# RMSNorm with repeat: the two halves of the first tile on two hardware queues, gamma behind the first half

## The chip, the cores and the metric

The kernel runs on one core of a Trainium2 chip. The metric is the device time of one execution in microseconds. Times inside an execution are counted from the start of its span, which is some 1.8 us shorter than the device time.

## The reference, cut to what matters

```
x: (8, 512, 2048) float32, gamma: (2048,) float32, R = 2
x_rep  = repeat(x, 2, axis=1)
rms    = sqrt(mean(x_rep**2, axis=-1) + 1e-6)
out    = x_rep / rms * gamma            # (8, 1024, 2048) float32
```

Each row of x is normalised, scaled by gamma, and written twice. 33.6 MB are read and 67.1 MB written.

## The kernel before

The 4096 rows are cut into eight tiles of 128 partitions by four rows. A tile's loads put the four rows (8 KB each) into the second half of a buffer of eight rows; ScalarE squares and sums each row and takes the root, VectorE scales the row by the reciprocal and gamma into its place, and then the rows are copied to their doubles. One store writes the eight rows of each partition (64 KB). There are three buffers, so three tiles are loaded at first, and later loads wait for stores.

```
    def load(i, eng, parts=1):
        y = rows.tile([P, K * R, D], f32, name="y")
        step = K // parts
        for k in range(0, K, step):
            at = K * (R - 1) + k
            eng.dma_start(out=y[:, at : at + step, :], in_=x_t[i, :, k : k + step, :])
        ys.append(y)
    ...
    load(0, nc.sync, parts=2)
    gamma_b = singles.tile([P, D], f32, name="gamma_b")
    cuts = [0, *range(D // 4, D + 1, D // 8)]
    for c0, c1 in zip(cuts, cuts[1:]):
        nc.scalar.dma_start(out=gamma_b[0:1, c0:c1], in_=gamma[c0:c1].partition_broadcast(1))
    nc.gpsimd.partition_broadcast(out_ap=gamma_b[:], in_ap=gamma_b[0:1, :])
    eps_t = singles.tile([P, 1], f32, name="eps_t")
    nc.vector.memset(eps_t, eps)
    load(1, nc.sync)
    load(2, nc.sync)
    ...
    loads_after = {2: (3, 4, 5), 4: (6, 7)}
    for i in range(ntiles):
        compute(i)
        store(i, 0, K)
        for j in loads_after.get(i, ()):
            load(j, nc.sync)
```

Gamma comes in seven pieces on ScalarE's queue, with nothing ahead of it there; all x traffic is on SP's queue; and the only transfers queued before the first store are the loads of tiles 0, 1 and 2.

## Time and profile before

| | before |
|---|---|
| device time, median | 239.7 us in three runs; 239.45 us over all six runs beside the changed kernel |
| span of the profiled run | 237.9 us |
| broadcast of gamma starts | 12.60 us |
| first store issued | 27.05 us |
| last load of tiles 0 to 2 complete | 33.0 us |
| last store packet ends | 236.8 us |

The busy shares, the chain and the queues are read in the prediction. Here is one more view of the kernel before, the table of waits on the compute engines: who waited for whom, us in total, how often, the longest.

```profile
POOL gamma_b L96 <- DMA y<-in_x_dram: 12.2, 1, 12.2
DVE y L74 <- POOL gamma_b L96: 3.0, 1, 3.0
```

The first of these lines is an example of a wait that is put down to the wrong one. It names x, as if the broadcast had waited for the first tile. The program makes the broadcast wait for gamma alone; gamma's last completion packet (the 4-byte packet that follows a transfer's data in the packet records) came at 12.02 and the broadcast started at 12.60, while SP's second half of x completed only at 12.63. The chain of waits, shown in the prediction, names gamma. When a view names an input that the instruction does not read, look up the packets.

### The profile page before, as it was taken

The page shows a single profiled execution, that of the slowest core. Times are in us where ns is not written, and L with a number is a line of the kernel's source. Part 1 is how long each engine was busy: PE and PEld are TensorE (multiplying, and loading weights), DVE is VectorE, ACT ScalarE, POOL GpSimd, SP SyncE. Part 2 cuts the span into 40 slices and gives each one's busy share as a digit, 9 for nine tenths or more (in the row PEclk, how much of TensorE's full clock was granted, in tenths as well). Part 3 has the DMA queues.
Part 4 walks back from the last instruction along what each step waited for, and adds up shares of the span by engine and source line. Part 5 has one row for each costly group of instructions (what it writes and reads, how often), then busy time and mean ns, then how long its engine had stood idle before and what let it go on. Part 6 is the DMA issues. An engine that isn't in the chain of part 4 may idle for free.

```text
span 237.9 us, 287 instructions
## 1 busy us (share of the span) xinstructions
DVE 96.5 (41%) x73; ACT 101.0 (42%) x106; POOL 2.5 (1%) x5
## 2 busy tenths in 40 slices
DVE  0049999960000000059999960000199990000000
ACT  2697999900000000099999920000599960000000
POOL 0030000000000000000000000000000000000000
DMA  7999998989899998999998999989998989999994
GB/s 265 436 446 441 441 441 353 530 353 496 386 452 430 397 485 353 441 441 441 441 518 364 464 419 430 452 369 430 435 518 364 518 364 485 397 452 430 408 474 176
DMA packets 2464, 100.69 MB, mean 423 GB/s; under 512 B 279, under 2 KB 285, under 8 KB 286
## 3 DMA queue, kind: packets, MB, share of 16 engines
q1 hardware_dynamic: 2448, 100.66, 98.5%
q14 instruction: 2, 0.02, 0.0%
q10 hardware_dynamic: 14, 0.01, 0.0%
HBM read 33.56 MB, written 67.11 MB: 423 GB/s over the span
## 4 chain that ended last, share of the span: by engine, by line
DMA 58%; ACT 12%; DVE 9%; issue 1%; POOLq 1%; ACTq 1%; SPq 0%
DMA y<-in_x_dram 33%; DMA out_dram<-y 21%; ACT sq L64 8%; DVE y L74 7%; DMA gamma_b<-in_gamma_dram 4%; ACT y L81 3%; DVE y L81 2%; ACT rms L68 1%; POOLq L136 1%; ACTq L95 1%; DVE rstd L73 0%; POOLq L96 0%; SPq L56 0%
## 5 line engine op out<-in xcount | busy, mean ns | idle before, releaser
L64 ACT ACTIVATE sq<-y 128x2048 f32<-128x2048 f32 x32 | 59.7, 1865 | 87.8 <-DMA y<-in_x_dram 87.8
L74 DVE SCALAR_TENSOR_TENSOR y<-y,rstd,gamma_b 128x2048 f32<-128x2048 f32 x32 | 75.3, 2352 | 4.1 <-POOL gamma_b L96 3.0
L73 DVE RECIPROCAL rstd<-rms 128x1 f32<-128x1 f32 x32 | 5.0, 158 | 94.6 <-ACT rms L68 94.3
L81 ACT COPY y<-y 128x4096 f32<-128x4096 f32 x8 | 28.7, 3590 | 1.4 <-DVE y L74 1.4
L81 DVE COPY y<-y 128x4096 f32<-128x4096 f32 x8 | 18.3, 2294 | 0.3
L68 ACT ACTIVATE rms<-ss,eps_t 128x1 f32<-128x1 f32 x32 | 9.4, 295 | 1.0
L64 ACT ACTIVATION_READ_ACCUMULATOR sq<-y 128x1 f32 x32 | 6.0, 187 | 0.0
L64 ACT ACT_TABLE_LOAD x1 | 1.3, 1283 | 3.0 <-issue 3.0
L96 POOL PARTITION_BROADCAST gamma_b<-gamma_b x1 | 2.3, 2294 | 12.2 <-DMA y<-in_x_dram 12.2
L68 ACT ACT_TABLE_LOAD x1 | 1.3, 1283 | 0.0
L98 DVE MEMSET eps_t<- 128x1 f32 x1 | 0.1, 59 | 0.8 <-PEq L125 0.8
L125 POOL MEMSET const-uint8-127<- 128x1 uint8 x1 | 0.1, 102 | 0.0
L125 POOL MEMSET const-bfloat16-1.0<- 128x1 bf16 x1 | 0.1, 101 | 0.0
L125 POOL MEMSET const-float32-0.0<- 128x1 f32 x1 | 0.1, 98 | 0.2 <-issue 0.2
L125 POOL MEMSET const-float32-1.0<- 128x1 f32 x1 | 0.1, 98 | 0.0
## 6 DMA issues: line engine op xcount, KB each, us to landing
y<-in_x_dram SPq DMA_DIRECT2D x7, 4096.0 KB, 14.6
y<-in_x_dram SPq DMA_DIRECT2D x2, 2048.0 KB, 7.4
out_dram<-y SPq DMA_DIRECT2D x8, 24.4
gamma_b<-in_gamma_dram ACTq DMA_DIRECT2D x6, 1.0 KB
gamma_b<-in_gamma_dram ACTq DMA_DIRECT2D x1, 2.0 KB
```

The source lines that it names most:

```text
L64: nc.scalar.activation(out=sq[:], in_=ys[i][:, K * (R - 1) + k, :], func=Act.Square, accum_out=ss[:])
L68: nc.scalar.activation(out=rms[:], in_=ss[:], func=Act.Sqrt, scale=inv_d, bias=eps_t[:])
L73: nc.vector.reciprocal(out=rstd[:], in_=rms[:])
L74: nc.vector.scalar_tensor_tensor(out=ys[i][:, R * k, :], in0=ys[i][:, K * (R - 1) + k, :], scalar=rstd[:], in1=gamma_b[:], op0=Alu.mult, o ...
L81: copy(out=y_r[:, k0:k1, 1, :], in_=y_r[:, k0:k1, 0, :])
L95: nc.scalar.dma_start(out=gamma_b[0:1, c0:c1], in_=gamma[c0:c1].partition_broadcast(1))
L96: nc.gpsimd.partition_broadcast(out_ap=gamma_b[:], in_ap=gamma_b[0:1, :])
L98: nc.vector.memset(eps_t, eps)
L125: nc = _bacc.Bacc("TRN2", target_bir_lowering=False, num_devices=1)
L136: with _tile.TileContext(nc) as tc:
```

## The change

The intent is to send the two halves of the first tile out at once, one from each hardware queue, so that neither waits for the other to be issued. Since ScalarE's queue now begins with a half, gamma stands behind that half on it.

```diff
-    def load(i, eng, parts=1):
+    def load(i, queues):
         y = rows.tile([P, K * R, D], f32, name="y")
-        step = K // parts
-        for k in range(0, K, step):
+        step = K // len(queues)
+        for k, eng in zip(range(0, K, step), queues):
             at = K * (R - 1) + k
             eng.dma_start(out=y[:, at : at + step, :], in_=x_t[i, :, k : k + step, :])
 ...
-    load(0, nc.sync, parts=2)
+    load(0, (nc.scalar, nc.sync))
 ...                                   (gamma's seven pieces follow on nc.scalar, as before)
-    load(1, nc.sync)
-    load(2, nc.sync)
+    load(1, (nc.sync,))
+    load(2, (nc.sync,))
 ...
-            load(j, nc.sync)
+            load(j, (nc.sync,))
```

## The prediction

> **What bounds the kernel now.** I read the page first: its busy shares, the strip of 40 slices, and the queues.
>
> ```profile
> DVE 96.5 (41%) x73; ACT 101.0 (42%) x106; POOL 2.5 (1%) x5
> ...
> DMA  7999998989899998999998999989998989999994
> ...
> HBM read 33.56 MB, written 67.11 MB: 423 GB/s over the span
> ```
>
> No compute engine reaches half the span, and the DMA strip is full from the second slice to the last but one. The bytes decide: a 64 KB store packet takes 2.418 us in the trace's packet records, so 16 engines move about 434 GB/s and 100.7 MB need 232 us of the 237.9. The other 6 us are the start (first data packet at 1.73 us), the ramp (first packets of 16 KB take 0.7 to 1.6 us, later ones 0.611) and the end. A change to the first tile can therefore matter in two ways only: a few tenths at the start, or a **hole in the DMA stream**.
>
> So I next asked where a hole could open. The chain of waits, cut to the first 28 us:
>
> ```profile
> 2.69 9.71 DMA gamma_b<-in_gamma_dram
> ...
> 12.55 2.35 POOLq L136
> 14.90 0.02 issue
> 14.92 2.35 DVE y L74
> ...
> 24.69 2.30 DVE y L81
> ...
> 27.05 25.77 DMA out_dram<-y
> ```
>
> Read it downwards: gamma's last piece lands, GpSimd broadcasts it, VectorE scales four rows and copies two, and at 27.05 the first store is issued. This chain, and not x, sets the first store. Meanwhile the DMA engines work off the loads of tiles 0, 1 and 2, which are all that is queued until that store; the packet records show their last completion packet at 33.0. The store was thus queued about 6 us before the loads ran out, and there was no hole.
>
> Two more views matter. The waits of the issuing sequencer SP show waits that no data explains:
>
> ```profile
> SPq L52 <- DMA y<-in_x_dram: 5.7, 1, 5.7
> ...
> SPq L52 <- DMA gamma_b<-in_gamma_dram: 0.9, 1, 0.9
> ```
>
> The second half of x was issued only at 2.03, after gamma's first piece had landed, and tile 1 at 8.11, after the first half had landed. In the trace the DMA issues count on eight semaphores used in turn, and a ninth issue waits for the first user of its semaphore. And the queues between 5.6 and 12.1 us:
>
> ```profile
> q1 hardware_dynamic: 186, 2.79, 100.0%
> q10 hardware_dynamic: 12, 0.01, 0.3%
> ```
>
> q1 is SP's queue, q10 that of ScalarE, with gamma alone on it. Six pieces of gamma took 6.5 us as 12 packets (a data packet and a 4-byte completion packet for each piece), from 5.65 to 12.02: between any two of them the engine moved one 16 KB packet of x, so a piece took 1.262 us, twice 0.611 and a little.
>
> **What the Trainium skill says.** "DMA: Bandwidth & Descriptors", section "Issuing engines are not separate DMA queues", says that DMAs issued from different engines run on the same 16 DMA engines and interleave, and that only issue time is saved. The trace agrees: with both queues active a packet of x still takes 0.611 us. The section "Queues, rings and completion order" says that each DMA engine goes round the queues that have work, a packet at a time; the alternation above is just that, and it is the key to my number. The section "Why a DMA increments its semaphore by 16 and not by 1" says that the engine count follows the slowest dimension; gamma's one-row pieces leave one data packet each, so they sit on one engine, again as recorded. "ScalarE: Activation LUTs", section "What ACT_TABLE_LOAD costs", gives 1283 ns, and the trace shows the same 1283 ns.
>
> **The change part by part.**
> *Bytes:* none added, none removed: 0 us.
> *Issue of the second half:* it goes out at 0.72 instead of 2.03. The engines then still had 16 KB packets of the first half until 7.3 us, so they never lacked work: gain about 0. The total of the loads still ends near 33 us.
> *First half:* with a half on each queue, the engines alternate between them. Both land near 12.5 instead of 8.1 and 13.0. ScalarE starts its first square about 4 us later, and possibly later still, because its last gamma issues may wait for a semaphore that the halves hold, with the 1.283 us table load behind them. But squares took only 2.2 us a row and were ahead of gamma; four of them need 9 us, so this path alone would move the first scaling to some 18.5: hidden.
> *Gamma:* this is the part that counts. Its 14 packets now stand behind the first half on ScalarE's queue, on one engine, and alternate with what SP has queued there: first what is left of the second half (0.61 us a packet), then tile 1 and tile 2, whose packets are 32 KB and take 1.213 us in the records. Before, 12 packets alternated with 16 KB ones.
> How late may gamma be? From its last packet (12.02) to the first scaling (14.92) is 2.90 us; from there to the store's issue (27.05) is 12.13, bound by VectorE; from an issue to its first packet I take 1.0 (0.72 to 1.73 at the start). Store data would start 16.0 us after gamma's last packet, and loads end at 33.0: gamma may land up to **17.0 us** for nothing. Beyond that each us opens a us of hole, and nothing later makes it up, since the DMA is full to the end.
> When does it land? By alternation, with the start at 1.77, 0.85 of ramp and 0.607 from packet to packet of 16 KB (1.21 for 32 KB):
> (a) Both halves arrive together: 16 packets end at 1.77 + 0.85 + 9.7 = 12.3. The 14 packets of gamma then alternate with 12 packets of 32 KB (two of the slots between go to completion packets): 14.5, and 0.3 for gamma itself: 27.1. Hole 27.1 + 16.0 - 33.0 = 10.1; 239.7 + 10 = **250**.
> (b) ScalarE's half comes slightly first. In the records five 16 KB packets of x preceded gamma's second piece, so some five packets can be ahead. The first half ends sooner, gamma passes the rest of the second half cheaply and meets only 8 packets of 32 KB: 12.3 + 9.7 + 0.3 = 22.3. Hole about 5.3; **245**.
> (c) SP's half comes first by as much: gamma starts some 5 us later and meets all of tiles 1 and 2, so it ends with the loads near 33. Hole about 16; **255.5**.
> The two first issues were 6 ns apart before (0.716 on ScalarE, 0.722 on SP), so I can't order them; I lean to (b), as gamma's first packet came ahead of x.
>
> **Rivals.**
> *A semaphore wait replaces the one removed.* If tile 1's load takes a semaphore held by one of the halves, it is issued only when that half lands, near 12.6. Then the queue is empty for about 1.5 us, gamma has its engine for itself and lands near 14, inside the 17.0: total about **241.5**. For it: such a wait was in the kernel before (5.7 us). Against it: in the old order the one-row pieces had taken the semaphores before tile 1, and SP was given its second half after all seven pieces; now a long transfer heads both queues, tile 1 should be among the first five to take one, and the pieces at the end should wait instead.
> *Hidden anyway.* If the engines served a short packet at once, gamma would land by 14 and only the start would change: 239.5. Against it: the strict alternation of 5.65 to 12.02.
> *ScalarE becomes the bound* of the first tile through its later squares: worked out above as 18.5 for the first scaling, against 19.9 where a hole would start. Hidden, but with little to spare.
> *Faster start.* Two queues fill the engines sooner: at most a part of the 0.85 of ramp.
>
> **Range and chances.** I give 0.12 to the rivals that leave no large hole (239 to 242), and of the rest some 0.4 to (b), 0.3 each to (a) and (c). The middle lies between (b) and (a): **248.0 us**, and 241.5 to 255.5 should hold it 8 times in 10. Slower by over 2% begins at 244.5: (a), (c) and most of (b), together 0.73. Within 2%: 0.25. Faster by over 2%: 0.02, as the whole time above the DMA's own 232 us is 6 us, most of it fixed.
>
> **What the profile would show.** Right: a 5 to 16 us stretch near 33 to 45 us with no DMA traffic; gamma's packets on ScalarE's queue from about 9 to 12 us on, 1.2 us apart, ending between 22 and 33; the first store issued 15.0 after the last of them; VectorE's first scaling waiting for the broadcast; both halves landing near 12; every later store shifted by the same amount, and no new gap after. Wrong: SP issuing tile 1 only after 12 us (the semaphore rival), gamma's packets close together, or a first store before 32 us. The number would be wrong most easily through the order in which the two halves reach the one engine that carries gamma.

## The result, and the profile after

The changed kernel takes 253.15 us (median of six runs, 252.7 to 253.31) against 239.45 us (six runs, 239.32 to 240.03). The ratio is 1.0564, 95% interval 1.055 to 1.0579.

The page of the changed kernel, in the lines that answer to those of before:

```profile
DVE 96.5 (38%) x73; ACT 101.1 (40%) x106; POOL 2.5 (1%) x5
...
DMA  7999900979979799699999998989999899899994
...
HBM read 33.56 MB, written 67.11 MB: 400 GB/s over the span
```

The engines did the same work (VectorE 96.5 us in both) and the same bytes moved, but two slices of the DMA strip, the sixth and seventh of 6.3 us each, are now empty. That is the hole. The stretches around it, first of the kernel before, then of the changed one (columns: stretch, length, busy us and instructions of VectorE, ScalarE, GpSimd, clock, mean DMA share, GB/s):

```profile
12.70:31.80 19.10, 16.66 (x12) 17.53 (x21) 2.19 (x1) 1.00 1.00 412
31.80:44.50 12.70, 12.49 (x12) 12.54 (x16) 0.00 (x0) 1.00 0.96 418
```

```profile
12.70:31.80 19.10, 0.41 (x2) 11.43 (x14) 2.29 (x1) 1.00 0.96 414
31.80:44.50 12.70, 12.52 (x10) 8.04 (x8) 0.00 (x0) 1.00 0.00 0
```

Up to 31.8 us both move the same bytes per second; then the changed kernel moves nothing for 12.7 us, while VectorE, which had been almost idle (0.41 us of work in 19.1), does the work that it had done before by then. The chain of waits of the changed kernel, cut to its first 50 us (start, length, what):

```profile
0.72 12.55 DMA y<-in_x_dram
...
13.55 15.51 DMA gamma_b<-in_gamma_dram
...
29.18 2.35 POOLq L137
31.53 0.03 issue
31.55 2.35 DVE y L74
```

Gamma takes the 15.5 us from 13.55 on, where it ended at 12.40 before; the broadcast and the first scaling follow as they did, but at 31.55 instead of 14.92. The waits say the same:

```profile
POOL gamma_b L97 <- DMA gamma_b<-in_gamma_dram: 28.8, 1, 28.8
ACT L64 <- DMA gamma_b<-in_gamma_dram: 13.8, 1, 13.8
DVE y L74 <- POOL gamma_b L97: 12.6, 1, 12.6
```

The second line is a rival that the experiments must deal with: ScalarE's own start was late too. Its last two pieces of gamma reuse the semaphores of the halves, were issued at 13.29 and 13.55 when those had landed, and its first square came at 15.14 instead of 8.12. Last, the queues of the changed kernel between 12.7 and 28.7 us (packets, MB, share of 16 engines):

```profile
q1 hardware_dynamic: 226, 6.85, 99.1%
q10 hardware_dynamic: 15, 0.01, 0.2%
```

ScalarE's queue needed 16 us for 8 KB: 14 packets of gamma and one completion packet of its half. The packet records show the pieces of gamma at 13.70, 16.21, 18.68, 21.14, 22.40, 24.87 and 27.34: 2.47 us apart, twice the 1.213 us of a 32 KB packet and a little. Only the step to 22.40 is 1.26, where one of the turns fell on a 4-byte completion packet of tile 1.

**The account.** From the first to the last packet of x or of the output, the mean idle time of a DMA engine rose from 0.8 to 13.45 us and its packet time from 234.2 to 235.2 us: 12.6 and 0.95, together the 13.6 by which the last packet ended later (236.76 to 250.35).

### The profile page after: what moved, and what is told of

Read it like the earlier page. It is cut to its first block, busy times and chain, and to the rows that moved or that the text cites. A ratio compares the mean times of both kernels' runs of the same rounds, so it can differ in the third digit from the quotient of the medians.

```text
span 251.5 us, 286 instructions
## 1 busy us (share of the span) xinstructions
DVE 96.5 (38%) x73; ACT 101.1 (40%) x106; POOL 2.5 (1%) x5
## 4 chain that ended last, share of the span: by engine, by line
DMA 51%; DVE 18%; ACT 11%; issue 1%; POOLq 1%; SPq 0%; ACTq 0%
DMA y<-in_x_dram 35%; DVE y L74 15%; DMA out_dram<-y 10%; ACT sq L64 8%; DMA gamma_b<-in_gamma_dram 6%; ACT y L81 3%; DVE y L81 3%; ACT rms L68 1%; POOLq L137 1%; DVE rstd L73 1%; SPq L56 0%; ACTq L96 0%; POOLq L97 0%; SPq L52 0%
## 5 line engine op out<-in xcount | busy, mean ns | idle before, releaser
L74 DVE SCALAR_TENSOR_TENSOR y<-y,rstd,gamma_b 128x2048 f32<-128x2048 f32 x32 | 75.3, 2352 | 13.7 <-POOL gamma_b L97 12.6
L81 ACT COPY y<-y 128x4096 f32<-128x4096 f32 x8 | 28.7, 3593 | 11.0 <-DVE y L74 11.0
```

Source lines behind the costliest of these rows:

```text
L74: nc.vector.scalar_tensor_tensor(out=ys[i][:, R * k, :], in0=ys[i][:, K * (R - 1) + k, :], scalar=rstd[:], in1=gamma_b[:], op0=Alu.mult, o ...
L81: copy(out=y_r[:, k0:k1, 1, :], in_=y_r[:, k0:k1, 0, :])
```

## The experiments

The theory: gamma is late because each of its packets takes turns with a packet of x, the first store is late because gamma is, and each us that the store is late past the end of the loads is a us without DMA traffic. Two rivals: that the halves on two queues cost the time by themselves, and that ScalarE's late start does. Every kernel gave the correct result. All were timed beside the kernel before on the same chip (239.45 to 239.52 us there); "broadcast" is the start of GpSimd's broadcast of gamma, "store" the issue of the first store, both from the timeline of the profiled run.

| kernel | broadcast | store | time, us |
|---|---|---|---|
| before | 12.60 | 27.05 | 239.45 |
| before, gamma in one piece | 2.36 | 24.16 | 239.71 |
| one queue, gamma in three pieces behind both halves | 13.37 | 27.82 | 239.72 |
| changed, gamma in seven pieces ahead of its half | 8.85 | 29.07 | 239.87 |
| changed, gamma in one piece | 15.38 | 29.84 | 240.15 |
| the same, and six spare loads | 15.32 | 31.06 | 240.55 |
| changed, gamma in two pieces | 17.87 | 32.32 | 242.56 |
| changed, gamma in three pieces | 20.56 | 35.02 | 244.78 |
| changed, tiles 1 and 2 loaded in halves | 21.07 | 35.53 | 245.18 |
| changed, gamma in five pieces | 24.29 | 38.76 | 248.58 |
| **changed (seven pieces)** | 29.22 | 43.68 | 253.15 |
| before, but gamma issued after the first square | 30.08 | 44.54 | 253.94 |

(Two more kernels, in which gamma is early and a half of x is late, come further below.) From three pieces down to the last row the store comes 9.52 us later and the time is 9.16 us longer: close to one for one. From the first row down to the spare loads the time moves by 1.1 us.

**Fewer pieces of gamma, all else as changed.** The bytes stay the same and so does the place in the queue; only the number of turns falls.

```diff
-    cuts = [0, *range(D // 4, D + 1, D // 8)]
+    cuts = [0, D]                                              # one piece
+    cuts = [0, D // 4, D]                                      # two
+    cuts = [0, D // 4, 5 * D // 8, D]                          # three
+    cuts = [0, D // 4, D // 2, 5 * D // 8, 3 * D // 4, D]      # five
```

> The changed kernel with gamma in one piece instead of seven; both halves still on two queues, gamma still behind the first half. Theory (late gamma opens the hole, one us for one us): the completion packet of the first piece came at 15.0 in the changed kernel, so gamma is complete near 15.0, store data could start at 15.0 + 15.1 + 0.8 = 30.9, the loads end at 31.8 to 32.2: no hole, 239.0 to 240.0 us. Rival (having the halves on two queues costs the time by itself): stays near 253. Second rival (ScalarE's late first square): ScalarE has no semaphore wait here, so it can not be told from the theory by this run; also near 239.5.

Measured 240.15 us, ratio 1.0032 (1.0013 to 1.0051). The halves are still on two queues and gamma still behind one: the rival of the two queues is refuted as the cause of the loss. All but 0.6 us of it is gone; the median lies 0.15 us above what was expected.

> Gamma in three pieces, all else as changed. ScalarE's issues wait for nothing (no semaphore is used twice among them). Theory: gamma complete near 19.9 (third completion packet of the changed kernel), 8.7 us before its 28.6, so 253.15 - 8.7 = 244.5 us, with a hole of about 4. Rival of ScalarE's late square: no waits, so as the one-piece kernel, near 239.5. Rival of the two queues: near 253.

Measured 244.78 us in one run (state unknown). The theory had 244.5.

> Gamma in five pieces. ScalarE's issues still wait for nothing. Theory: gamma complete near 23.7, 4.9 us before the 28.6 of seven pieces, so 248.2 us with a hole of about 8. Rival of ScalarE's late square: as one and three pieces, near 239.5. Rival of the two queues: near 253.

Measured 248.58 us in one run (state unknown). The theory had 248.2. In these kernels none of ScalarE's issues waits for anything, and its first square starts at 13.1 to 13.3 in all of them, so ScalarE's start cannot make the difference between 240, 245 and 249.

> Gamma in two pieces, all else as changed; it looks for the knee between one piece (no hole) and three (244.8). Theory: gamma complete near 17.4, store data 15.9 later at 33.3, a hole of 1.5 over loads that end at 31.8: 3 pieces less 2.5 us, that is 242.3, or less if the slower packets seen after a hole do not come: 241.0 to 242.5. If the free slack reached to 17.0 as the prediction had it: 240.0 to 240.6.

Measured 242.56 us, ratio 1.0133 (1.011 to 1.0157), with runs between 242.0 and 243.6, wider than the others; the median is just above the 242.5 of the theory. The hole in its trace is 1.55 us. The knee lies between one and two pieces, lower than the prediction had it.

**ScalarE late, gamma early.** Gamma in one piece, and behind it six loads into a tile that nothing reads, which make ScalarE's issues wait as in the changed kernel.

```diff
-    cuts = [0, *range(D // 4, D + 1, D // 8)]
-    for c0, c1 in zip(cuts, cuts[1:]):
-        nc.scalar.dma_start(out=gamma_b[0:1, c0:c1], in_=gamma[c0:c1].partition_broadcast(1))
+    nc.scalar.dma_start(out=gamma_b[0:1, :], in_=gamma.partition_broadcast(1))
+    spare = singles.tile([1, 3 * D // 4], f32, name="spare")
+    for c0 in range(D // 4, D, D // 8):
+        nc.scalar.dma_start(out=spare[0:1, c0 - D // 4 : c0 - D // 8], in_=gamma[c0 : c0 + D // 8].partition_broadcast(1))
```

> Gamma in one piece, followed on ScalarE's queue by six loads of 1 KB into a tile that nothing reads, so that ScalarE's issues wait for the halves as in the changed kernel and its first square starts near 15.1, but gamma is complete near 15.0. Theory: ScalarE's delay is hidden but for little: first scaling at 18.8, store issued near 31.0, 239.3 to 240.3 us. Rival (ScalarE's late start causes the loss): near 253.

Measured 240.55 us, ratio 1.0046 (1.0031 to 1.0062). The waits of this kernel show that ScalarE was held as long as in the changed kernel, and gamma was not:

```profile
POOL gamma_b L98 <- DMA gamma_b<-in_gamma_dram: 14.9, 1, 14.9
ACT L64 <- DMA spare<-in_gamma_dram: 13.7, 1, 13.7
```

Tile 2 was issued as late as in the changed kernel, too (15.25 against 15.41). So these waits add 0.4 us to the kernel with gamma in one piece, and the two together cost 1.0 us over the kernel before, 0.25 more than the expectation allowed. ScalarE's wait was hidden but for little, as the prediction said (first scaling at 18.93, worked out as 18.5).

**Late gamma alone.** The kernel before, with both halves on SP's queue, and gamma issued by ScalarE after its first square.

```diff
-    for c0, c1 in zip(cuts, cuts[1:]):
-        nc.scalar.dma_start(out=gamma_b[0:1, c0:c1], ...)
-    nc.gpsimd.partition_broadcast(out_ap=gamma_b[:], in_ap=gamma_b[0:1, :])
 ...
         for k in range(K):
-            scale(i, k, square(i, k))
+            rms = square(i, k)
+            if i == 0 and k == 0:
+                gamma_in()          # the lines taken out above
+            scale(i, k, rms)
```

> The kernel before (both halves on SP's queue, as there) with one thing changed: ScalarE issues the seven pieces of gamma after its first square instead of at the start, so gamma meets the 32 KB packets of tiles 1 and 2. Theory: gamma complete between 28 and 33, store issued 15.1 later, a hole of 12 to 16: 251 to 256 us, though no half is on another queue. Rival (halves on two queues cost the time): 239.5.

Measured 253.94 us, ratio 1.0606 (1.0588 to 1.0624), the loss of the changed kernel without any half on another queue. ScalarE's first square is at 8.05 here, as early as before. Its wait for gamma and its DMA strip:

```profile
POOL gamma_b L101 <- DMA gamma_b<-in_gamma_dram: 29.7, 1, 29.7
```

```profile
DMA  7999900979799797999999989979999799997995
```

The same two slices are empty. Late gamma is enough, and neither rival is needed.

**Smaller neighbours.** The changed kernel with tiles 1 and 2 loaded in halves: gamma keeps its 14 packets and its place, but takes turns with 16 KB packets.

```diff
-    load(1, (nc.sync,))
-    load(2, (nc.sync,))
+    load(1, (nc.sync, nc.sync))
+    load(2, (nc.sync, nc.sync))
```

> The changed kernel with the loads of tiles 1 and 2 issued as two halves each, so that the packets beside gamma are 16 KB instead of 32 KB; gamma has its 14 packets in the same place. Theory (a gamma packet waits for one packet of x, whatever its size): pitch of a piece 1.26 instead of 2.47, gamma complete near 12.7 + 14 x 0.62 = 21.3, hole near 5.5: 245 to 246.5 us. Rival (what counts is gamma's place in the queue and not the size of the neighbours): near 253.

Measured 245.18 us, ratio 1.0239 (1.0223 to 1.0254). Its pieces of gamma come at 12.81, 14.11, 15.37, 16.63, 17.29, 18.56 and 19.82, some 1.26 us apart but for one step of 0.66, where a turn fell on a completion packet of x. The queues between 12.7 and 20.6 us:

```profile
q1 hardware_dynamic: 224, 3.41, 100.7%
q10 hardware_dynamic: 14, 0.01, 0.3%
```

The same 14 packets of gamma pass in half the time because as many packets of x beside them carry half the bytes. So a turn goes by packets, here of 16 or 32 KB, and not by bytes.

**Behind x, but on the same queue.** Three pieces of gamma behind both halves, all on SP's queue.

```diff
-    load(0, (nc.scalar, nc.sync))
+    load(0, (nc.sync, nc.sync))
-    cuts = [0, *range(D // 4, D + 1, D // 8)]
+    cuts = [0, D // 4, 5 * D // 8, D]
-        nc.scalar.dma_start(out=gamma_b[0:1, c0:c1], in_=...)
+        nc.sync.dma_start(out=gamma_b[0:1, c0:c1], in_=...)
```

> Gamma in three pieces behind both halves, but halves, gamma and the tiles after it all on SP's one queue, so that gamma has no other queue to take turns with. Compare with three pieces on ScalarE's queue (244.8). Theory (the turns with 32 KB packets cost the time, not the place behind x): gamma complete near 13.2, store data could start near 29, no hole: 239.3 to 240.3 us. Rival (gamma behind x is late in any case): near 244.8.

Measured 239.72 us, ratio 1.0010 (0.9996 to 1.0023), against 244.78 for the same three pieces on ScalarE's queue. SP's issues (start, length from the first to the last, what):

```profile
0.73 0.86 SPq L52 DMA_DIRECT2D y<-in_x_dram  x2
1.64 0.88 SPq L96 DMA_DIRECT2D gamma_b<-in_gamma_dram  x3
2.56 0.84 SPq L52 DMA_DIRECT2D y<-in_x_dram  x2
```

Gamma stands behind the whole first tile, and its first packet starts at 12.23, when that tile is through. But then its pieces follow one another, with tile 1 behind them in the same queue, and the broadcast starts at 13.37. Standing behind x costs nothing here; taking turns with what is queued elsewhere does.

**Gamma ahead of its half, seven pieces.**

```diff
-    load(0, (nc.scalar, nc.sync))
     gamma_b = singles.tile([P, D], f32, name="gamma_b")
     cuts = [0, *range(D // 4, D + 1, D // 8)]
     for c0, c1 in zip(cuts, cuts[1:]):
         nc.scalar.dma_start(out=gamma_b[0:1, c0:c1], ...)
+    load(0, (nc.scalar, nc.sync))
```

> The halves on two queues as in the changed kernel, but the seven pieces of gamma ahead of the first half on ScalarE's queue. Theory: gamma alternates with 16 KB packets of the second half and is complete by 11 to 14, no hole; the first half is issued later and lands later (up to 15), still inside the slack of 5 us: 239 to 241 us. Rival (two queues for the halves): near 253.

Measured 239.87 us, ratio 1.0015 (0.9998 to 1.0031). With gamma ahead the loss is gone, though both halves are still on two queues. But the edit moved more than gamma: tile 1 was issued only at 9.21, as its semaphore was that of SP's half; so the half on ScalarE's queue had no 32 KB packets beside it and was complete at 12.46. Whether the order alone would have done it, this run does not show; the next one bears on it.

**Gamma ahead, in one piece: a miss.** This should have been as good.

```diff
-    cuts = [0, *range(D // 4, D + 1, D // 8)]
+    cuts = [0, D]                              # on top of the edit above
```

> Halves on two queues, gamma in one piece ahead of the first half. Theory: gamma complete near 2, off the path; the second half is what the first store waits for; DMA full: 239.0 to 240.0, within 0.3% of the kernel before. If two queues fill the engines sooner there would be up to 0.8 us to gain: 238.7.

Measured 243.6 us, ratio 1.0172 (1.0158 to 1.0186). Gamma is not the cause: its broadcast starts at 2.45. ScalarE's first square is (the bracket is its idle time and what ended it):

```profile
17.83 1.88 ACT L64 ACTIVATE sq<-y 128x2048 f32<-128x2048 f32 x1 [14.88 <-DMA y<-in_x_dram]
```

It waits for the first half. That half was issued at 1.26, behind gamma, 0.54 us after SP's half at 0.72, and with few semaphores in use SP issued tile 1 at 1.16, waiting for nothing. SP's half was complete at 10.1; the first half then took turns with 32 KB packets of tile 1 and was complete only at 17.4. The store went out at 33.86 and the hole was 3.1 us. To test that, the halves were exchanged, so that the late one is the half that is needed later:

```diff
-    load(0, (nc.scalar, nc.sync))
+    load(0, (nc.sync, nc.scalar))
```

> The kernel that missed (gamma in one piece first, halves on two queues: 243.6) with the halves exchanged: the first half on SP's queue, the second behind gamma on ScalarE's. Theory: in the run that missed, the half behind gamma was issued 0.5 us after the other, fell some packets behind, then took turns with 32 KB packets of tile 1 and landed at 17.4 instead of 12.7; ScalarE's first square needs the first half, so the store came at 33.9 and a hole of 3.1 opened. With the halves exchanged the late one is the second, which is needed only from the third square on: first half lands near 10, second near 17.4, the last square then ends near 22, the store goes out near 27.5: no hole, 239.3 to 240.3 us. If something else in that kernel cost the 4 us: 243 to 244.

Measured 239.75 us, ratio 1.0016 (1.0001 to 1.0032). ScalarE's first square:

```profile
10.43 1.88 ACT L64 ACTIVATE sq<-y 128x2048 f32<-128x2048 f32 x1 [7.48 <-DMA y<-in_x_dram]
```

The first half was complete at 10.06 and the second at 17.3; the store was issued at 27.50, and there was no hole. So the same turns that delay gamma can delay a half of x.

**Gamma early in the kernel before.** If an earlier first store were worth something, gamma in one piece in the kernel before should show it.

```diff
-    cuts = [0, *range(D // 4, D + 1, D // 8)]
+    cuts = [0, D]                              # in the kernel before
```

> The kernel before with gamma in one piece. Theory: gamma complete near 2 instead of 12 and the first store earlier by some us, but the DMA has loads queued until 33 in any case, so nothing is gained: 239.0 to 239.8. If an earlier first store were worth anything, up to 2 us less.

Measured 239.71 us, ratio 1.0010 (0.9997 to 1.0024). The store was issued 2.9 us earlier and nothing was gained, as the loads were still queued. No version beat the kernel before: it has no hole to close, and these edits do not touch its bytes.

## Why the prediction was right

It said 248.0 us, between 241.5 and 255.5, slower; it is 253.15, inside the range, 5 us above the point.

- **The bound and the way of the loss: right.** The DMA is the bound, the only way to lose much was a hole between the last load and the first store, and gamma opened it. The empty stretch, the pieces of gamma two 32 KB packets apart, the store 15.07 us after gamma's last completion packet (28.61 to 43.68; predicted 15.0), VectorE waiting for the broadcast, and both halves landing together (12.72) were all as foretold. Gamma's first packet moved at 13.70, later than the 9 to 12 foretold. The range was 14 us wide, as the order of the halves could not be told; that the number fell inside it says less than these lines do.
- **Where the chances were put: half right.** Of the three orders it leaned to (b), ScalarE's half first, 245 us. The trace shows (a), the halves packet by packet in turn, for which it had 250. The weighting of the orders (248.0 against 250) is 2.0 of the 5.15 us; the two terms below add 1.5 and 2.1, and 0.45 comes off, as 250 was rounded up from 249.8 and the kernel before took 239.45, not 239.7. That the order matters as much as it said was shown by the run that missed: there an issue 0.54 us later, behind a gamma in one piece, made that half land at 17.4 instead of 12.7.
- **The term "gamma complete at 27.1" of (a) was 1.5 too small.** It came at 28.61: of the two turns that it gave to completion packets, one went to a 32 KB packet before the first piece (which moved at 13.70), so 13 of these passed instead of 12, 1.2 us; the other 0.3 is the sum of the small terms. (The prediction's reading of the kernel before, "between any two of them the engine moved one 16 KB packet of x", has one exception: a piece came 0.66 us after the one before, at 7.57, where the turn fell on a completion packet of x. For (a) it allowed for such turns.)
- **The term "17.0 us for nothing" was 2.1 too large.** It took the end of the loads from the kernel before, 33.0. There the first store was already queued, and packets of tile 2 took 0.94 us per engine longer than their 1.213; in the changed kernel they took no longer, and the loads end at 31.5 to 32.2, in the middle 31.8. (With gamma in one piece the store was queued at 29.84, some 2 us before the loads ended, and they took no longer either; so not every store behind the loads lengthens them. How early it must be queued was not tested.) The first store packet came 0.84 after the issue, not 1.0. A hole thus opens when gamma is complete after 15.9, that is 31.8 less 15.07 and 0.84. Packets near the later turns between loads and stores then took 0.95 us more than before; with that, a late gamma costs its time of completion less about 14.9, and 10.1 + 1.5 + 2.1 = 13.7, which is what the medians show. The knee bears this out roughly: gamma complete at 14.9 costs 0.6 us, at 17.3 (two pieces) 3.1, where the sum gives 0 and 2.4.
- **The rivals.** Tile 1 waited for no semaphore (issued at 1.16); tile 2 waited for gamma's first piece until 15.4, while tile 1 was still moving, so it cost nothing. "Hidden anyway" is refuted by the pitch of 2.47. ScalarE's late start is hidden but for about 0.4 to 1 us, as the run with spare loads shows. A faster start was not there: the first packet came at 1.74 and 1.73.

One thing stays open: why the packets near the later turns take 0.95 us more in all kernels whose first store came late. No run was made for it, but the traces narrow it. The excess over 2.418 us for each 64 KB store packet is 0.07 us per engine in the kernel before, 0.19 with gamma in one piece (store issued at 29.84), 0.95 with the spare loads (31.06) and 0.96 in the changed kernel. With the spare loads the engines idled for only 0.2 us between loads and stores. So the excess does not grow with the hole, and it is most of the 1.0 us that the spare loads cost.

## What to carry to other kernels

Before moving a transfer to another queue, ask what stands in the other queues while it is served: a small transfer there advances by one packet for each packet of its neighbour, so many small pieces beside 32 KB rows crawl, and one piece, or the same pieces in the same queue as the bulk, do not. In a kernel that is bound by DMA, find the last moment at which the first store may be issued without a hole, and check every input of that store against it, gamma as well as x. Take that moment from a run in which no store is queued while the loads are served: here the loads then ended at 31.8 us, and not at the 33.0 that the kernel before shows.

## What the Trainium skill lacked or had wrong

- "DMA: Bandwidth & Descriptors", section "Issuing engines are not separate DMA queues", says that DMAs from several engines interleave and that only issue time is saved. It lacks that interleaving can cost: three pieces of gamma took 244.78 us on ScalarE's queue and 239.72 on SP's, and seven took 253.15.
- The same page, section "Queues, rings and completion order", gives the turn as a packet of typically 9 to 17 descriptors. In these traces each row of 16 or 32 KB was a turn by itself, and so was a completion packet of 4 bytes: gamma's pieces were 1.26 or 2.47 us apart, two such turns. It doesn't say that the length of a turn follows the neighbour's row.
- No page has how far one queue gets ahead when the other is issued a little later: five 16 KB packets before gamma's second piece in the kernel before, and an issue 0.54 us later made a half of x land 4.7 us later (17.4 against 12.7).
